# Splitting the rows once, early, for every gather, and adding them onto the sum during the routing

## The chip, the cores and the metric

The kernel runs on one core of a Trainium2 chip. The metric is the device time of one execution in microseconds, as the median of several runs. The core has five engines that run their own instruction streams and wait for each other through semaphores: TensorE (PE, matrix products; PEld is its weight loads), VectorE (DVE), ScalarE (ACT), GpSimd (POOL) and SyncE (SP), which here issues nearly all DMA transfers. Matrix products land in PSUM, eight banks of 128 partitions by 512 float32; everything else lives in SBUF.

## What is computed

One encoder layer on 256 rows of 1024 features, then a mixture of 16 small experts. Cut to what matters:

```python
h = h + (g_sb * y_sb + g_ret * y_ret) @ w_out[layer]      # output projection: the "rows" are this h
hn = rms_norm(h, norm_ffn_g[layer])
# inside the mixture, xt is hn, 256 x 1024
p_group, g_sel = lax.top_k(group_probs, 1)                 # best of 4 groups
top_vals, top_idx = lax.top_k(in_group, TOP_K_IN_GROUP)    # best 2 of its 4 experts
for e in range(N_EXPERTS):
    hidden = jax.nn.silu(xt @ w_exp_gate[e]) * (xt @ w_exp_up[e])
    y = y + combine[:, e:e + 1] * (hidden @ w_exp_down[e])
h = h + y
return rms_norm(h, norm_final_g)
```

Each row goes to two of the 16 experts.

## The kernel before

**Stages.** The input projections, attention, retention and the output projection come first. The output projection `wo` is worked off in 8 units of 256 columns by half the depth; its result is added to `xt`, a tile of 256 rows by 1024 columns in float32 (the rows). Columns 0 to 255 are finished first, then 256 to 511, and so on; the four pieces are numbered n = 0 to 3, and `tb` (0 or 1) is the half of the rows. The last piece is worked out by hand after the unit loop, together with the routing: the row norm (`row_norm`, its power on POOL), the comparison of the logits (`choose`), the ranks of the rows in each expert (small products into the PSUM tile `rp`) and the one-hot table `pt0` that says which row goes to which place.

**Experts.** They are worked off in 8 pairs, i = 0 to 7. For a pair there are three products, each of 32 matmuls of 512 columns on four weight tiles r = 0 to 3: `gate(i)`, `up(i)` and `down(i)`, L1000 and L1034 in the profile. I write g3, u3, d3 for those of pair 3. Every one of the three writes one PSUM bank, which is then read: g by the `silu` on ACT (L1010), u by the product with it on DVE (L1015), d by `hilo`, a copy on ACT (L563) and after it a subtraction on DVE (L564). The order is g0, u0, then for i = 1 to 3 g(i), d(i-1), u(i); then the second gather, d3, g4, u4; then g5, d4, u5, g6, d5, u6, g7, u7; then d6, d7 and the final norm. The banks come from a pool `g` of two one-bank tiles, so a product writes into the bank that was read after the product before the last one.

**Gathers.** The rows of eight experts are fetched into `xgt` by products with the one-hot table. For the first half of the experts this happens in float32 straight from `xt` (`gather_two`, L933): two pairs' rows (i = 0) in four pieces around g0, the other two pairs' (i = 1) in pieces around g1. For the second half it is done from `hn`, the rows split in a high and a low part of the faster matmul type (`gather`, L922). The split is made by `rows_in_parts` (ACT L944, DVE L945) during u2.

**Sum.** Four PSUM banks `F` collect the experts' results by `scatter` (L1044), and the rows themselves by `rows_onto` (L1051), in u3.

**Weights.** `pump` issues the transfer of the next weight tile (1 MiB) on SP whenever one of 25 SBUF slots is free; the table `LIMIT` says how many tiles may be on their way by which unit of the first part. Tiles from the 38th on are expert weights. `xt`, `xgt` and the two tiles of `hn` hold a slot each. `keep_warm` (L205) are products without a use, ahead of the first gather. `values_load` reads the largest number of rows of an expert into a register of every engine; it is read at the end, to choose whether one pass is enough.

Of the kernel before, what the change touches and what calls it, by code (L numbers as in the profile page):

```python
# [17 lines left out]
P = 128  # L18
T = 256
# [79 lines left out]
def layer(ctx: ExitStack, tc, cst, dec, prm, x, w_in, w_gate, w_sb_out, w_ret_out,  # L99
# [8 lines left out]
    banks = ExitStack()  # L108
    banks.__enter__()
    ps_z = banks.enter_context(tc.tile_pool(name="ps_z", bufs=1, space=PSUM))  # L110
    pp = {"d": banks.enter_context(tc.tile_pool(name="ps_d", bufs=4, space=PSUM)),
          "m": banks.enter_context(tc.tile_pool(name="ps_m", bufs=2, space=PSUM))}
# [312 lines left out]
    def squares(n, eng, tbs=range(NB)):  # L425
        cs = wo_cols[n]
        for tb in tbs:
            j, v, a = bank("d")[:, 0:cs.stop - cs.start], xt[:, tb, cs], ssh[:, n, tb:tb + 1]
# [329 lines left out]
    give(A["yrh"], A["yrl"])  # L758
    lp = bank2()
    nu = len(units)  # L760
    while i < nu - 1:
        set_limit(i)
        mm_unit(i)
        i += 1
        if i == n1 + 3:
            transpose_h(0)
            squares(0, act)
        if i == n1 + 4:
            logits(lp, 0)
        if i == n1 + 5:  # L770
            transpose_h(1)
            squares(1, act)
        if i == nu - 2:
            give(splits[(i - 1) % 3])
            logits(lp, 1)
        if i == nu - 1:
            give(splits[(i - 1) % 3], comb[0])
            transpose_h(2)
            squares(2, act)
            for n in (1, 2):  # L780
                pool.tensor_tensor(ssh[:, 0, :], ssh[:, 0, :], ssh[:, n, :], op=ALU.add)
            pool.tensor_scalar(ssh[:, 0, :], ssh[:, 0, :], 1.0 / D, EPS, op0=ALU.mult, op1=ALU.add)
# [11 lines left out]
    rp = bank("d")  # L794
# [77 lines left out]
    pt0 = small([P, NB, 4, CAP], F32R, "pt")  # L872
    onehot_of(pt0, 0, 0, ranks, 0, 2)
# [3 lines left out]
    keep_warm(1)  # L877
    onehot_of(pt0, 0, 1, ranks, 0, 2)
    give(comb[1], splits[i % 3])
    xgt = take([P, KC, T])  # L880
    limit[0] = 10 ** 6
    pump()
    dve.tensor_copy(rank, ranks)
    for tb in range(NB):
        onehot_of(pt0, 0, tb, rank, 2, 4)
# [11 lines left out]
    banks.close()  # L897
    banks = ExitStack()
    banks.__enter__()
    ctx.push(banks)  # L900
    pp["f"] = banks.enter_context(tc.tile_pool(name="ps_f", bufs=4, space=PSUM, reuse_waits="tile"))
    pp["g"] = banks.enter_context(tc.tile_pool(name="ps_g", bufs=2, space=PSUM, reuse_waits="tile"))
    pp["x"] = banks.enter_context(tc.tile_pool(name="ps_x", bufs=2, space=PSUM, reuse_waits="tile"))

# [4 lines left out]
    y2, work, gs = [], {}, {}  # L909
    F = [[bank("f") for _ in range(NB)] for _ in range(2)]  # L910
# [4 lines left out]
    def gather(k, pt, cs=range(4)):  # L915

        for c2 in cs:
            ps = bank("x").rearrange("p (c s) -> p c s", c=2)
            for h in range(2):
                for c in range(2):  # L920
                    for tb in range(NB):
# [6 lines left out]
    def gather_two(i, pt, c2):  # L928

        ps = bank("x")[:, 0:2 * P].rearrange("p (c s) -> p c s", c=2)  # L930
        for c in range(2):
            for tb in range(NB):
                pe.matmul(ps[:, c, :], xt[:, tb, features(c2, c)],  # L933
                          pt[:, tb, 2 * i:2 * i + 2].rearrange("p e s -> p (e s)").bitcast(F32),
                          start=c == 0 and tb == 0, stop=c == 1 and tb == 1, skip_group_check=True)
        tt(xgt[:, 2 * c2:2 * c2 + 2, i * P:i * P + P], ps,
           fp[:, 2 * c2:2 * c2 + 2][:, :, None].to_broadcast([P, 2, P]), op=ALU.mult)

    def rows_in_parts():
        hi, lo = hn  # L940
        for q in range(2):
            for tb in range(NB):
                cs = slice(512 * q, 512 * q + 512)
                act.activation(hi[:, tb, cs], xt[:, tb, cs], AF.Copy)  # L944
                tt(lo[:, tb, cs], xt[:, tb, cs], hi[:, tb, cs].bitcast(F32), op=ALU.subtract)  # L945
        give(xt)
# [8 lines left out]
    def tables(i):  # L955

        pb = work["pb"].rearrange("p (b e s) -> p b (e s)", b=NB, e=2)
        gp = bank("x")[:, 0:9]
# [7 lines left out]
        ps = bank("x", BF16)  # L966
# [4 lines left out]
    def convert(key):  # L971
        if len(hn) < 2 and key in (("u", 2, 0), ("u", 2, 2)):
            hn.append(take([P, NB, D], F32R))
            if len(hn) == 2:
                rows_in_parts()

    def after(key):
        drop(key)
        if not work and key == ("u", 0, 0):
            w = take([P, 2048])  # L980
            work.update(b=w[:, 0:512], ht=[w[:, 512 + 512 * k:1024 + 512 * k].rearrange("p (f s) -> p f s", f=4)
                                           for k in range(2)],
                        pb=w[:, 1536:1664].bitcast(BF16), S=[small([P, T], F32R, "S")])
        if not y2 and key == ("u", 0, 3):
            w = take([P, 2048], F32R)
            y2.append(w[:, 0:1024].rearrange("p (h n) -> p h n", h=2))
            work["S"].append(w[:, 1024:1024 + T])
        convert(key)
        pump()
# [14 lines left out]
    def gate(i, hook=None):  # L1004
        g = bank("g")
        proj(i, "g", g, hook)
        return g
# [4 lines left out]
    def up(i, hook=None):  # L1012
        u = bank("g")
        proj(i, "u", u, hook)
        stt(work["b"], u, gs[i][:, 0:1], work["b"], op0=ALU.mult, op1=ALU.mult)  # L1015

    def hidden(i):
        hps = bank("x").rearrange("p (f s) -> p f s", f=4)
# [4 lines left out]
    def down(i, hook=None):  # L1023

        y, ht = bank("g"), work["ht"][i % 2]
# [13 lines left out]
    def scatter(i, tb, first=False, last=False):  # L1039

        for h in range(2):
            for q in range(2):
                r = slice(64 * q, 64 * q + 64)
                pe.matmul(F[q][tb], work["S"][i % 2][r, tb * P:(tb + 1) * P], y2[0][r, h, :],  # L1044
                          start=first and h == 0, stop=last and h == 1, skip_group_check=True)

    def rows_onto():
        for tb in range(NB):
            for h in range(2):
                for q in range(2):  # L1050
                    pe.matmul(F[q][tb], identr, hn[h][:, tb, 512 * q:512 * q + 512], start=False, stop=False,  # L1051
                              skip_group_check=True)
# [42 lines left out]
    def head(first):  # L1095

        pt = pt0 if first else onehot(0)
        fetch = (lambda c2: gather_two(0, pt, c2)) if first else (lambda c2: gather(0, pt, [c2]))
        parts = shares() if first else iter(())
        fetch(0)  # L1100

        def ahead(r):
            if r < 3:
                fetch(r + 1)
            next(parts, None)
# [10 lines left out]
        if first:  # L1116
            gather_two(1, pt, 0)
            gather_two(1, pt, 1)
        for i in range(1, NP):
# [6 lines left out]
            def in_up(r):  # L1126
                if r == 2 and i < NP - 1:
                    for tb in range(NB):
                        scatter(i - 1, tb, first and i == 1)
                    if first and i == 3:  # L1130
                        rows_onto()
# [13 lines left out]
            if first and i == 1:  # L1145
                gather_two(1, pt, 2)
                gather_two(1, pt, 3)
# [21 lines left out]
    def final_gain(q):  # L1169
        if len(final) < 2:  # L1170
            if not final:
                final.append(take([P, 2048])[:, 0:D])
            ps = bank("x")
# [31 lines left out]
    most = nc.values_load(cnt[0:1, 0:1], min_val=0, max_val=T)  # L1205
# [3 lines left out]
    with tc.If(most <= CAP) as fits:  # L1209
# [41 lines left out]
```

## Time and profile before

| what | us |
|---|---|
| median of 3 runs (lowest to highest) | 467.12 (466.46 to 469.71) |
| the profiled execution, its own time | 468.08 |
| its span in the trace | 466.1 |

The durations below come from the profiled execution, which is 0.96 us above the median; 1.98 us of its time lie outside its span. The first gather begins at 251.97 us and the final norm at 455.7 us; between them the experts take 204 us.

### The profile page before, as it was taken

How to read it: one execution, taken by the hardware profiler on the slowest of the kernel's cores; microseconds unless marked ns; L12 is line 12 of the kernel's file. 1: busy time of each engine (PE TensorE's matmuls, PEld its weight loads, DVE VectorE, ACT ScalarE, POOL GpSimd, SP SyncE). 2: the span in 40 equal slices, each digit the busy share in tenths (PEclk: the TensorE clock that was granted, in tenths of full speed). 3: DMA queues.
4: the chain of work that ended last, by engine and by line, in shares of the span. 5: the costliest groups of instructions: out<-in, count | busy, mean ns of one | idle time of the engine just before them, and what ended most of it. 6: DMA issues, size and time to landing. Idle time of an engine off the chain costs nothing.

```text
span 466.1 us, 6780 instructions
## 1 busy us (share of the span) xinstructions
PE 446.3 (96%) x2735; PEld 301.4 (65%) x2735; DVE 187.5 (40%) x353; ACT 165.7 (36%) x239; POOL 21.8 (5%) x36
## 2 busy tenths in 40 slices
PE   7899999999999999999998999999989999999991
PEld 6699777888899999999996444333344333333330
DVE  4756487553466855678525320103012110101003
ACT  3643688885644654444431021012101010101113
POOL 2300110110002100000000000000000000000000
PEclk9999999999999999999998999999999999999996
DMA  8999985249202289995994989999999999999952
GB/s 283 353 383 392 389 258 160 84 148 317 68 8 85 92 279 380 408 377 183 356 358 190 333 323 373 412 408 411 408 409 408 410 408 409 408 410 409 409 231 96
DMA packets 58036, 142.48 MB, mean 306 GB/s; under 512 B 3344, under 2 KB 23952, under 8 KB 57872
## 3 DMA queue, kind: packets, MB, share of 16 engines
q1 hardware_dynamic: 57568, 141.35, 80.8%
q10 hardware_dynamic: 432, 0.65, 0.5%
q8 instruction: 23, 0.38, 0.3%
q14 instruction: 13, 0.11, 0.1%
HBM read 140.93 MB, written 1.05 MB: 305 GB/s over the span
## 4 chain that ended last, share of the span: by engine, by line
PE 93%; DVE 2%; ACT 1%; DMA 1%; issue 1%; POOL 1%; DVEq 0%
PE p L1000 24%; PE p L294 20%; PE p L1034 12%; PE p L281 8%; PE p L284 7%; PE p L282 7%; PE p L933 2%; PE p L1044 2%; PE z L577 1%; PE p L922 1%; PE p L1020 1%; DMA b<-in_x 1%; PE p L205 1%; PE p L679 1%; PE p L620 1%
## 5 line engine op out<-in xcount | busy, mean ns | idle before, releaser
L253 DVE TENSOR_TENSOR b<-b,b 128x1024 fp32r<-128x1024 f32 x72 | 88.7, 1240 | 71.8 <-ACT b L251 70.2
L1000 PE MATMUL p<-b,b 128*64 128x512 f32 x512 | 115.1, 596 | 0.0
L294 PE MATMUL p<-b,b 128*128 128x512 f32 (+1 forms) x504 | 102.4, 359 | 0.9 <-ACT b L251 0.7
L251 ACT ACTIVATE b<-b 128x1024 fp32r<-128x1024 f32 x72 | 75.5, 1056 | 77.3 <-PE p L282 47.8
L294 PEld LDWEIGHTS p<-b,b 128*128 128x128 f32 x504 | 82.3, 189 | 15.2 <-ACT b L251 1.3
L1000 PEld LDWEIGHTS p<-b,b 128*64 128x64 f32 x512 | 35.0, 137 | 66.3 <-issue 63.0
L281 PE MATMUL p<-b,b 128*128 128x256 f32 x288 | 71.6, 286 | 0.0
L282 PE MATMUL p<-b,b 128*128 128x256 f32 x288 | 70.7, 283 | 0.0
L1034 PE MATMUL p<-b,b 128*64 128x512 f32 x256 | 56.7, 594 | 0.0
L281 PEld LDWEIGHTS p<-b,b 128*128 128x128 f32 x288 | 55.1, 191 | 0.5
L282 PEld LDWEIGHTS p<-b,b 128*128 128x128 f32 x288 | 55.2, 192 | 0.0
L284 PE MATMUL p<-b,b 128*128 128x256 f32 x288 | 41.1, 283 | 0.0
L1034 PEld LDWEIGHTS p<-b,b 128*64 128x64 f32 x256 | 18.0, 137 | 35.1 <-issue 33.1
L564 DVE SCALAR_TENSOR_TENSOR b<-p,b 128x512 fp32r<-128x512 f32 (+1 forms) x12 | 7.2, 599 | 75.2 <-ACT b L563 75.2
L284 PEld LDWEIGHTS p<-b,b 128*128 128x128 f32 x288 | 37.4, 192 | 0.0
L1015 DVE SCALAR_TENSOR_TENSOR b<-p,share,b 128x512 f32<-128x512 f32 x8 | 6.0, 750 | 55.9 <-PE p L1000 55.9
L563 ACT ACTIVATE b<-p 128x512 fp32r<-128x512 f32 (+1 forms) x12 | 6.3, 522 | 53.4 <-PE p L1034 52.8
L969 ACT ACTIVATE b<-p 128x256 fp32r<-128x256 bf16 x4 | 1.5, 385 | 37.4 <-PE p L968 37.4
L969 ACT ACTIVATE S<-p 128x256 fp32r<-128x256 bf16 x4 | 1.5, 383 | 36.8 <-PE p L968 36.8
L1010 ACT ACTIVATE b<-p,share 128x512 f32<-128x512 f32 x8 | 5.5, 687 | 21.2 <-PE p L1000 21.2
L1021 ACT ACTIVATE b<-p 128x512 f32<-128x512 f32 x8 | 4.8, 597 | 22.9 <-PE p L1020 22.9
L933 PEld LDWEIGHTS p<-pt,b 128*128 128x128 f32 x64 | 7.9, 196 | 4.9 <-issue 4.9
(175 smaller groups left out, 342.8 us busy)
## 6 DMA issues: line engine op xcount, KB each, us to landing
b<-in_w_exp_gate SPq DMA_DIRECT2D x64, 512.0 KB, 10.2
b<-in_w_exp_up SPq DMA_DIRECT2D x64, 512.0 KB, 10.2
b<-in_w_exp_down SPq DMA_DIRECT2D x31, 1024.0 KB, 11.5
b<-in_w_in SPq DMA_DIRECT2D x17, 1024.0 KB, 14.4
b<-in_w_gate SPq DMA_DIRECT2D x8, 1024.0 KB, 5.3
b<-in_w_ret_out SPq DMA_DIRECT2D x4, 1024.0 KB, 5.0
b<-in_w_out SPq DMA_DIRECT2D x4, 1024.0 KB, 11.5
b<-in_w_sb_out SPq DMA_DIRECT2D x2, 1024.0 KB, 8.8
```

Of the source, the lines that this page charges most:

```text
L251: act.activation(hi, raw, AF.Copy)
L253: tt(lo, raw, hi.bitcast(F32), op=ALU.subtract)
L281: pe.matmul(ps, wh[:, k, cs], h[:, k, :], start=k == 0, stop=False)
L282: pe.matmul(ps, wh[:, k, cs], l[:, k, :], start=False, stop=False)
L284: pe.matmul(ps, wl[:, k, cs], h[:, k, :], start=False, stop=k == nk - 1)
L294: pe.matmul(ps[tb], kth(a, k)[:, tb * P:(tb + 1) * P], b[:, j, :], start=n == 0 and k == 0, stop=n == 2 and k == KC - 1)
L563: act.activation(hi, src, AF.Copy)
L564: stt(lo, src, 1.0, hi.bitcast(F32), op0=ALU.mult, op1=ALU.subtract)
L933: pe.matmul(ps[:, c, :], xt[:, tb, features(c2, c)], pt[:, tb, 2 * i:2 * i + 2].rearrange("p e s -> p (e s)").bitcast(F32), start=c == 0 a ...
L1000: pe.matmul(ps[64 * j:64 * j + 64, :], xgt[:, c, o:o + 64], w[:, j, k, :], start=c == 0, stop=c == KC - 1)
L1034: pe.matmul(y[64 * q:64 * q + 64, :], ht[:, f, 64 * j:64 * j + 64], w[:, k, 512 * q:512 * q + 512], start=r == 0 and k == 0, stop=r == 3 a ...
L1044: pe.matmul(F[q][tb], work["S"][i % 2][r, tb * P:(tb + 1) * P], y2[0][r, h, :], start=first and h == 0, stop=last and h == 1, skip_group_c ...
```

## The change

- `row_parts(n, tb)` splits a piece of the rows as soon as the output projection has delivered it: a copy to the high part on ACT and a subtraction for the low part on POOL, eight times in all, 128 by 256 each. `rows_in_parts`, `gather_two` and the slots taken in u2 are gone; `xgt` and the two tiles of `hn` take their slots at the start of `wo` instead, and `LIMIT` is lower there by two or three tiles.
- All gathers use the split rows, for four pairs of experts at a time: the first one stands wholly ahead of and inside g0.
- `rows_onto(q, tb)` adds the rows to the sum `F` during the routing, where the `keep_warm` products stood. It opens the sum, so `scatter` no longer does.
- The PSUM pools stay open to the end. `F` are the four `d` banks; `bank("m")` takes the place of `bank("x")`; the ranks `rp` are a corner of `lp`; and the three products of a pair write in turn into the two halves `lp[:, 0]` and `lp[:, 1]` of the one two-bank tile `lp` (`bank_g`).
- `squares` writes its unused output to SBUF. `pump` is let loose before the ranks are known, and `values_load` stands after g2.

```diff
-    (59, 48), (61, 49), (63, 50), (64, 53), (65, 54), (67, 55), (69, 56), (70, 57), (71, 59),
+    (59, 48), (61, 49), (63, 50), (65, 51), (67, 52), (69, 53), (70, 54), (71, 56),
...
+    def row_parts(n, tb):
+
+        hi, lo = [t[:, tb, wo_cols[n]] for t in hn]
+        act.activation(hi, xt[:, tb, wo_cols[n]], AF.Copy)
+        pool.tensor_tensor(lo, xt[:, tb, wo_cols[n]], hi.bitcast(F32), op=ALU.subtract)
...
     give(A["yrh"], A["yrl"])
+    xgt = take([P, KC, T])
+    junk = xgt[:, 0:2, :]
+    hn.extend(take([P, NB, D], F32R) for _ in range(2))
     lp = bank2()
...
             transpose_h(2)
             squares(2, act)
+            for tb in range(NB):
+                row_parts(2, tb)
             for n in (1, 2):
                 pool.tensor_tensor(ssh[:, 0, :], ssh[:, 0, :], ssh[:, n, :], op=ALU.add)
...
-    rp = bank("d")
+    rp = lp[:, 0, 64:96]
...
+    give(comb[1], splits[i % 3])
+    F = [[bank("d") for _ in range(NB)] for _ in range(2)]
+
+    def rows_onto(q, tb):
+        for h in range(2):
+            pe.matmul(F[q][tb], identr, hn[h][:, tb, 512 * q:512 * q + 512], start=h == 0, stop=False,
+                      skip_group_check=True)
+
     best, norm = choose(0), row_norm(1)
     next(best)
     next(norm)
+    row_parts(3, 0)
     next(best)
     next(norm)
     next(best)
+    row_parts(3, 1)
+    give(xt)
+    limit[0] = 10 ** 6
+    pump()
+    rows_onto(0, 0)
     logits(lp, 3, [1])
     pe.matmul(rp[:, 0:8], tri, either[:, 0, :], start=True, stop=True)
     pe.matmul(rp[:, 8:16], ones, either[:, 0, :], start=True, stop=False)
-    keep_warm(6)
+    rows_onto(0, 1)
+    rows_onto(1, 0)
     list(choose(1))
...
-    banks.close()
...
-    pp["g"] = banks.enter_context(tc.tile_pool(name="ps_g", bufs=2, space=PSUM, reuse_waits="tile"))
...
+    def bank_g():
+        turn[0] ^= 1
+        return lp[:, turn[0], :]
...
-        fetch = (lambda c2: gather_two(0, pt, c2)) if first else (lambda c2: gather(0, pt, [c2]))
...
+            if first and i == 2:
+                most.append(nc.values_load(cnt[0:1, 0:1], min_val=0, max_val=T))
```

The change moves instructions at three places that matter below. The first is TensorE at the borders u1 to g2, g2 to d1 and d1 to u2. A row is the line, the operation, what it writes and reads, and the semaphores that it waits for (DMAHW: a weight tile has landed; a count of ACT or DVE: an instruction there is done). Before:

```order
L1000 MATMUL p_2734<-b_2300,b_2460 64x512 x2
L1000 MATMUL p_2771<-b_2345,b_2460 64x512 [waits DMAHW0_49,PE_49]
...
L1000 MATMUL p_2771<-b_2542,b_2460 64x512 x2
L1034 MATMUL p_2817<-b_2560,b_2596 64x512 [waits DMAHW0_49,Activation_49]
...
L1034 MATMUL p_2817<-b_2604,b_2596 64x512 x3
L1000 MATMUL p_2845<-b_2622,b_2460 64x512 [waits DMAHW4_49,Activation_49]
```

After (line numbers are those of the changed kernel: L990 is g and u, L1024 is d):

```order
L990 MATMUL z_2087<-b_2419,b_2084 64x512 x2
L990 MATMUL z_2087<-b_2422,b_2084 64x512 [waits DMAHW0_49,DVE_49]
...
L990 MATMUL z_2087<-b_2527,b_2084 64x512 x2
L1123 TENSOR_LOAD cnt_2456 [waits DVE_49]
L1024 MATMUL z_2087<-b_2550,b_2567 64x512 [waits DMAHW0_49,Activation_49]
...
L1024 MATMUL z_2087<-b_2593,b_2567 64x512 x3
L990 MATMUL z_2087<-b_2607,b_2084 64x512 [waits DMAHW4_49,DVE_49]
```

All products now write one tile, `z_2087` (`lp`), and the counts have other owners. In the program before, the count at the start of d1 is that of the copy of the hidden rows at r = 2 of g2, and the count at the start of u2 that of the `silu` of g2; g2 waits for no other engine. In the changed program g2 waits for the DVE product of u1 (L1005, the L1015 of before), d1 for the `silu` of g2 (L1000, before L1010), and u2 for the subtraction of `hilo` of d1 (L568, before L564): each for the read of the product just ahead of it.

The second place is POOL in the routing. `ssh` are the sums of squares, `rh` the power that the row norm needs, for tb = 0 and 1. Before:

```order
L781 TENSOR_TENSOR ssh_91<-ssh_91 128x2 [waits Activation_49]
L781 TENSOR_TENSOR ssh_91<-ssh_91 128x2 [waits Activation_49,Pool_49]
L782 TENSOR_SCALAR ssh_91<-ssh_91 128x2 [waits Pool_49]
L820 TENSOR_TENSOR rh_2351<-rh_2351,mhalf_84 128x1 [waits DVE_49] x2
L1205 TENSOR_LOAD cnt_2470 [waits DVE_49]
```

After (L436 is the subtraction of `row_parts`; the first row here is that of n = 2, tb = 1):

```order
L436 TENSOR_TENSOR b_2086<-b_74,b_2085 128x256 [waits DMAHW5_49,DVE_49,Activation_49]
L794 TENSOR_TENSOR ssh_91<-ssh_91 128x2
L794 TENSOR_TENSOR ssh_91<-ssh_91 128x2 [waits Pool_49]
L795 TENSOR_SCALAR ssh_91<-ssh_91 128x2 [waits Pool_49]
L833 TENSOR_TENSOR rh_2351<-rh_2351,mhalf_84 128x1 [waits DVE_49]
L436 TENSOR_TENSOR b_2086<-b_74,b_2085 128x256 [waits Activation_49]
L833 TENSOR_TENSOR rh_2351<-rh_2351,mhalf_84 128x1 [waits DVE_49]
L436 TENSOR_TENSOR b_2086<-b_74,b_2085 128x256 [waits Activation_49]
```

The subtractions of n = 2 now stand ahead of the sums, and that of n = 3, tb = 0 ahead of the second power.

The third place is TensorE from the last ranks to g0. Before:

```order
L205 MATMUL p_2454<-ones_78 128x128
L1205 TENSOR_LOAD cnt_2470 [waits DVE_49]
L933 MATMUL p_2505<-pt_2449,b_74 128x128 [waits PE_49]
L933 MATMUL p_2505<-pt_2449,b_74 128x128 [waits DVE_49]
L933 MATMUL p_2505<-pt_2449,b_74 128x128 x2
L933 MATMUL p_2512<-pt_2449,b_74 128x128 x4
L1000 MATMUL p_2511<-b_1472,b_2460 64x512 [waits DMAHW4_49,DVE_49]
```

After (L879 is `rows_onto`, L939 the gather from the split rows):

```order
L879 MATMUL p_2405<-b_2085,identr_80 128x512 [waits Activation_49]
L879 MATMUL p_2405<-b_2086,identr_80 128x512 [waits Pool_49]
L939 MATMUL p_2461<-pt_2444,b_2085 128x256 [waits PE_49]
L939 MATMUL p_2461<-pt_2444,b_2085 128x256
L939 MATMUL p_2461<-pt_2444,b_2086 128x256 x2
L939 MATMUL p_2461<-pt_2444,b_2085 128x256 [waits DVE_49]
L939 MATMUL p_2461<-pt_2444,b_2085 128x256
L939 MATMUL p_2461<-pt_2444,b_2086 128x256 x2
L939 MATMUL p_2471<-pt_2444,b_2085 128x256 [waits PE_49]
```

The load of the register is gone from here, and the rows' last piece is put onto the sum ahead of the gather.

## Rows read from the trace of the kernel before

**Rows 1.** The page: busy time of the engines, and the chain by engine.

```profile
PE 446.3 (96%) x2735; PEld 301.4 (65%) x2735; DVE 187.5 (40%) x353; ACT 165.7 (36%) x239; POOL 21.8 (5%) x36
...
PE 93%; DVE 2%; ACT 1%; DMA 1%; issue 1%; POOL 1%; DVEq 0%
```

**Rows 2.** Stretches: us, busy PE, PEld, DVE, ACT, POOL, clock, DMA share, GB/s.

```profile
400.00:420.00 20.00, 19.87 (x100) 6.93 (x98) 1.20 (x5) 2.26 (x4) 0.00 (x0) 1.00 1.03 409
...
450.00:451.00 1.00, 1.00 (x6) 0.29 (x4) 0.00 (x0) 0.00 (x0) 0.00 (x0) 1.00 0.14 57
```

**Rows 3.** The timeline at u2, d2 and d6: products, and reads of those before them.

```profile
313.29 3.60 PE L1000 MATMUL p<-b,b 128*64 128x512 f32 x16
313.57 0.60 ACT L563 ACTIVATE b<-p 128x512 fp32r<-128x512 f32 x1 [6.24 <-PE p L1034]
...
314.20 0.69 DVE L564 SCALAR_TENSOR_TENSOR b<-p,b 128x512 fp32r<-128x512 f32 x1 [11.54 <-ACT b L563]
...
329.51 7.04 PE L1034 MATMUL p<-b,b 128*64 128x512 f32 x32
329.73 0.69 ACT L1010 ACTIVATE b<-p,share 128x512 f32<-128x512 f32 x1 [3.00 <-PE p L1000]
...
437.86 3.60 PE L1034 MATMUL p<-b,b 128*64 128x512 f32 x16
...
438.13 0.75 DVE L1015 SCALAR_TENSOR_TENSOR b<-p,share,b 128x512 f32<-128x512 f32 x1 [12.08 <-PE p L1000]
```

**Rows 4.** The timeline at the last scatter, which waits for the read of d7.

```profile
454.45 0.69 DVE L564 SCALAR_TENSOR_TENSOR b<-p,b 128x512 fp32r<-128x512 f32 x1 [7.31 <-ACT b L563]
...
455.19 0.96 PE L1044 MATMUL p<-b 64*128 64x512 f32 x6 [0.23 <-DVE b L564]
```

**Rows 5.** The timeline at the second half of u0.

```profile
267.32 3.65 PE L1000 MATMUL p<-b,b 128*64 128x512 f32 x16
...
267.83 1.28 ACT L1010 ACT_TABLE_LOAD   x1
...
269.12 0.69 ACT L1010 ACTIVATE b<-p,share 128x512 f32<-128x512 f32 x1
```

**Rows 6.** Weight loads of g and u, by form: busy us, mean ns.

```profile
L1000 PEld LDWEIGHTS p<-b,b 128*64 128x64 f32 x512 | 35.0, 137 | 66.3 <-issue 63.0 <-DMA b<-in_w_exp_up 1.3 <-DMA b<-in_w_exp_gate 0.7
```

**Rows 7.** The chain that ended last: start us, us, what; gathers, rows, the last product.

```profile
270.97 2.08 PE p L933 x16
...
341.11 2.05 PE p L1051 x8
...
347.93 2.42 PE p L922 x16
...
351.12 2.20 PE p L922 x16
...
448.47 5.33 PE p L1034 x24
```

**Rows 8.** The timeline of the routing, to the first gather.

```profile
242.82 0.19 POOL L782 TENSOR_SCALAR ssh<-ssh 128x2 f32<-128x2 f32 x1
...
244.02 0.16 DVE L819 SCALAR_TENSOR_TENSOR rh<-ssh 128x1 f32<-128x1 f32 x1 [0.46 <-DVE p L432]
...
246.50 0.55 POOL L820 TENSOR_TENSOR rh<-rh,mhalf 128x1 f32<-128x1 f32 x1 [1.69 <-DVE rh L819]
...
251.97 2.12 PE L933 MATMUL p<-pt,b 128*128 128x128 f32 x16 [1.41 <-DVE cnt L895]
```

**Rows 9.** Nearest forms to the split on ACT and POOL: busy us, mean ns.

```profile
L395 ACT ACTIVATE b<-b 128x256 fp32r<-128x256 f32 x8 | 3.2, 403 | 2.1 <-DVE b L389 2.1
...
L504 POOL TENSOR_TENSOR b<-b,b 128x512 fp32r<-128x512 f32 x3 | 4.1, 1372 | 7.9 <-ACT b L501 7.9
```

**Rows 10.** Stretches where TensorE stood still at times; columns as in rows 2.

```profile
247.50:250.90 3.40, 3.06 (x32) 2.79 (x29) 1.96 (x10) 0.00 (x0) 0.00 (x0) 0.50 0.79 311
...
455.00:459.00 4.00, 0.96 (x6) 0.48 (x6) 2.34 (x8) 3.10 (x9) 0.84 (x2) 1.00 0.02 4
```

More of the change, by code (lines that the diff above doesn't have):

```diff
@@ L107, in layer @@
     sm = ctx.enter_context(tc.tile_pool(name="sm", bufs=1))
[L108 to L112, printed above, removed]
+    ps_z = ctx.enter_context(tc.tile_pool(name="ps_z", bufs=1, space=PSUM))
+    pp = {"d": ctx.enter_context(tc.tile_pool(name="ps_d", bufs=4, space=PSUM)),
+          "m": ctx.enter_context(tc.tile_pool(name="ps_m", bufs=2, space=PSUM))}
     ctx.enter_context(tc.manual_schedule())
@@ L427, in squares @@
         for tb in tbs:
-            j, v, a = bank("d")[:, 0:cs.stop - cs.start], xt[:, tb, cs], ssh[:, n, tb:tb + 1]
+            j, v, a = junk[:, tb, :], xt[:, tb, cs], ssh[:, n, tb:tb + 1]
             if eng is act:
@@ L772, in layer @@
             squares(1, act)
+            for tb in range(NB):
+                row_parts(1, tb)
         if i == nu - 2:
@@ L779, in layer @@
             squares(2, act)
+            for tb in range(NB):
+                row_parts(2, tb)
             for n in (1, 2):
@@ L876, in layer @@
     pe.matmul(rp[:, 16:24], ones, either[:, 1, :], start=False, stop=True)
[L877 to L882, printed above, removed]
+    rows_onto(1, 1)
+    onehot_of(pt0, 0, 1, ranks)
     dve.tensor_copy(rank, ranks)
-    for tb in range(NB):
-        onehot_of(pt0, 0, tb, rank, 2, 4)
     sel = small([P, NB, 4], F32, "sel")
@@ L908, in layer @@
     cmb = small([P, NB, NP, 3, 3], BF16, "cmb")
-    y2, work, gs = [], {}, {}
-    F = [[bank("f") for _ in range(NB)] for _ in range(2)]
+    y2, work, gs, turn = [], {}, {}, [0]
+    def bank_g():
+        turn[0] ^= 1
+        return lp[:, turn[0], :]
     def features(c2, c):
@@ L917, in gather @@
         for c2 in cs:
[L918 to L921, printed above, removed]
+            ps = bank("m").rearrange("p (c s) -> p c s", c=2)
+            for tb in range(NB):
+                for h in range(2):
+                    for c in range(2):
                         pe.matmul(ps[:, c, :], hn[h][:, tb, features(c2, c)], pt[:, tb].rearrange("p e s -> p (e s)"),
@@ L926, in gather @@
                fp[:, 2 * c2:2 * c2 + 2][:, :, None].to_broadcast([P, 2, 2 * P]), op=ALU.mult)
[L928 to L946, printed above, removed]
     def places(i):
@@ L957, in tables @@
         pb = work["pb"].rearrange("p (b e s) -> p b (e s)", b=NB, e=2)
-        gp = bank("x")[:, 0:9]
+        gp = bank("m")[:, 0:9]
         for tb in range(NB):
@@ L965, in tables @@
             tt(g[r, 0:1], g[r, 2 + j:3 + j], g[r, 1:2], op=ALU.mult)
-        ps = bank("x", BF16)
+        ps = bank("m", BF16)
         for tb in range(NB):
@@ L969, in tables @@
         act.activation(work["S"][i % 2], ps[:, 0:T], AF.Copy)
[L971 to L975, printed above, removed]
     def after(key):
@@ L1004, in gate @@
     def gate(i, hook=None):
-        g = bank("g")
+        g = bank_g()
         proj(i, "g", g, hook)
@@ L1012, in up @@
     def up(i, hook=None):
-        u = bank("g")
+        u = bank_g()
         proj(i, "u", u, hook)
@@ L1017, in hidden @@
     def hidden(i):
-        hps = bank("x").rearrange("p (f s) -> p f s", f=4)
+        hps = bank("m").rearrange("p (f s) -> p f s", f=4)
         for f in range(4):
@@ L1023, in down @@
     def down(i, hook=None):
-        y, ht = bank("g"), work["ht"][i % 2]
+        y, ht = bank_g(), work["ht"][i % 2]
         for r in range(4):
@@ L1037, in down, with scatter @@
         hilo(y2[0][:, 0, :], y2[0][:, 1, :], y)
-    def scatter(i, tb, first=False, last=False):
+    def scatter(i, tb, last=False):
         for h in range(2):
@@ L1044, in scatter @@
                 pe.matmul(F[q][tb], work["S"][i % 2][r, tb * P:(tb + 1) * P], y2[0][r, h, :],
[L1045 to L1052, printed above, removed]
+                          start=False, stop=last and h == 1, skip_group_check=True)
     def shares():
@@ L1097, in head @@
         pt = pt0 if first else onehot(0)
-        fetch = (lambda c2: gather_two(0, pt, c2)) if first else (lambda c2: gather(0, pt, [c2]))
         parts = shares() if first else iter(())
-        fetch(0)
+        gather(0, pt, [0])
         def ahead(r):
             if r < 3:
-                fetch(r + 1)
+                gather(0, pt, [r + 1])
             next(parts, None)
@@ L1115, in head @@
         up(0, early)
-        if first:
-            gather_two(1, pt, 0)
-            gather_two(1, pt, 1)
         for i in range(1, NP):
@@ L1128, in in_up @@
                     for tb in range(NB):
-                        scatter(i - 1, tb, first and i == 1)
-                    if first and i == 3:
-                        rows_onto()
+                        scatter(i - 1, tb)
                 if r == 2 and i == NP - 1:
@@ L1144, in head @@
             silu(i, g)
-            if first and i == 1:
-                gather_two(1, pt, 2)
-                gather_two(1, pt, 3)
+            if first and i == 2:
+                most.append(nc.values_load(cnt[0:1, 0:1], min_val=0, max_val=T))
             if i != 4 and i < NP - 1:
@@ L1172, in final_gain @@
                 final.append(take([P, 2048])[:, 0:D])
-            ps = bank("x")
+            ps = bank("m")
             for k in range(4):
@@ L1203, in finish @@
             sp.dma_start(out[0, tb * P:(tb + 1) * P, halves[1]], o[:, tb, halves[1]])
-    most = nc.values_load(cnt[0:1, 0:1], min_val=0, max_val=T)
+    most = []
     head(True)
@@ L1208, in layer @@
     kept = (dict(raws), dict(held), list(free))
-    with tc.If(most <= CAP) as fits:
+    with tc.If(most[0] <= CAP) as fits:
         tail()
```

9 lines of the change are left out of this document (2 added, 7 removed).

## The prediction

> **What bounds the kernel now.** I read the page first. TensorE is busy 96% of the span and 93% of the chain that ended last is its work [rows 1], so a time is won or lost where TensorE's own queue gets shorter or stands still. Next I read the stretches of the expert phase for the transfers. From 400 to 420 us the DMA engines are as full (share 1.03, 409 GB/s) as TensorE; they run dry just after 450 us [rows 2], and the last quarter of d7, the last 8 of the 24 matmuls of its row, starts a third of 5.33 us before their end at 453.8, at 452.0 us [rows 7]. So the weights arrive only 1 to 2 us ahead of their use: TensorE bounds the kernel, and the transfers stand right behind it. Third, the timeline at the borders between the products of a pair. Here the reader should look at start times: u2 starts at 313.29 while ACT begins to read d1 only at 313.57 and DVE ends at 314.89; d2 starts at 329.51 while the silu of g3 runs from 329.73; d6 starts at 437.86 while DVE reads u7 from 438.13 [rows 3]. No product waits for the read of the one before it.
>
> **The new waits.** This is where the change decides. In the order of the changed program every product of a pair writes a half of one tile, `lp`, and its first matmul waits for the read of the other half just ahead of it. The two halves are two banks, so the data don't ask for it; the wait is in the program all the same, and a read of a product can't be done before the product is. What one costs is read from rows 3 as the end of the read, less the time at which the next product starts today. From the end of a read to the matmul that waits for it pass 0.05 us (455.14 to 455.19) [rows 4].
> - After d, before u (or g4, d7): hilo ends at 314.89, plus 0.05, less 313.29: 1.65 us. Seven such borders (u1, u2, u3, g4, u5, u6, d7): 11.5 us.
> - After g, before d (or u4, u7): the silu ends at 330.42, plus 0.05, less 329.51: 0.96 us. Seven (d0, d1, d2, u4, d4, d5, u7): 6.7 us.
> - After u, before g (or d6): the product ends at 438.88, plus 0.05, less 437.86: 1.07 us. Seven (g1, g2, g3, g5, g6, g7, d6): 7.5 us.
> - Once, in the middle of u0: its third quarter waits for the silu of g0, which stands behind a table load. Today TensorE goes on at 267.32 and the silu ends at 269.81 [rows 5]; 2.54 us.
>
> The sum is 28.3 us, all on the path, since behind the waiting matmul stands the whole of TensorE's queue, and SP's next weight transfers wait for slots that this queue frees. Bounds: at least the reads' own durations count (1.29, 0.69 and 0.75 us seven times [rows 3], and 1.97 for the load and the silu [rows 5]), 21.1 us; at most each of the 22 restarts also pays a weight load that is covered today, 0.14 us [rows 6], 31.4 us. I take 28.3, because rows 3 show the very borders.
>
> **What the gathers give back.** Removed are eight pieces of `gather_two`: 2.12 us for the first two [rows 8] and 2.08 for each further two [rows 7], 8.4 us, all on the chain. Added are four pieces of `gather`, as the two later pairs of pieces show it: half of 2.42 to half of 2.20 each [rows 7], together 4.6. The result is 3.8 us less. The rows onto the sum leave u3: 2.05 us less [rows 7]. Where they go, TensorE waits for the routing, so there they replace warm-up products and cost nothing as long as POOL is in time. The split itself leaves ACT and DVE in u2, where neither is on the path; no gain.
>
> **The routing.** Eight copies on ACT at 0.40 us (the form is in the trace) and eight subtractions on POOL, 128 by 256; the nearest row is 128 by 512 at 1.37 us [rows 9], so 0.69 to 1.37. Five of the eight are hidden beside the last units of `wo`. Three are not. Those of n = 2 stand ahead of the sums of squares: today the sums end at 243.01 and DVE asks for them at 244.02 [rows 8]; two copies and two subtractions (the second copy beside the first subtraction) put 1.8 us ahead of them and the first sum, 0.3, no longer lies earlier, so they end near 245.1, a delay of 1.1 for DVE. The next subtraction stands ahead of the second power and, behind its own copy, adds some 0.5, so that the power begins near 248.1 instead of 246.50 [rows 8]. Against these 1.6 us stands TensorE's wait of 1.41 us for the largest count ahead of the first gather, which is gone [rows 8]; the register is now read at the start of d1, beside the wait for the silu. I put the routing at nought, with bounds of 2 us less (POOL covered, the whole wait saved) and 3 us more (1.37 us a subtraction).
>
> The lower table and the slots taken early put the stock of weights three tiles lower until the routing and one lower after it. At 409 GB/s [rows 2] a tile of 1 MiB takes 2.56 us, but TensorE, some 20 us late by the end, doesn't notice; without the new waits it would be the next bound. The output of `squares` in SBUF and the earlier `pump` hide beside TensorE's queue too.
>
> **Sum.** 28.3 - 3.8 - 2.05 + 0 = 22.4 us more. On the profiled execution's 468.08 us that is 490.5; it stands 0.96 above the median of 467.12, so the forecast for the median is 489.5. By the bounds: 21.1 - 3.9 - 2.05 - 2 = 13 more, and 31.4 - 3.7 - 2.05 + 3 = 28.6 more: 480 to 496.
>
> **Rivals.** *The waits cost nothing* (faster). If TensorE ran from half to half as it runs from bank to bank today, its queue would be 5.9 us shorter, and the transfers would become the bound: they end just after 450 us and the last quarter of d7 follows at 452.0 [rows 2, 7], so 1 to 2 us are to be had, plus or minus one tile's 2.56 us for the changed stock. That gives 465, and 463 to 468 with the stock. It decides if the wait is met before TensorE's queue gets there, which would need reads shorter than TensorE's run-ahead of 0.2 to 0.3 us [rows 3]; they are 0.69 and more. For it speaks that the two halves are different banks, as they are today. The Trainium skill, "PSUM — Partial Sum Buffer", section "PSUM bank collisions raise a hardware error", asks only that accesses be guarded by bank and quadrant, and its summary advises to read a different bank while a matmul runs. The trace of before agrees (rows 3 show such reads beside matmuls), and by that rule alone a reader would forecast this rival's 465; but the rule says what the chip needs, and the program waits for more. I give it 5 in 100, and 3 in 100 to something in between, within 1%.
>
> *The clock falls* (slower still). In the routing TensorE's granted clock went to 0.50 of full, 1.2 of 2.4 GHz, for the 3.4 us from 247.5 [rows 10], after stretches with short products and waits. If each of seven pairs brought one such spell, at half speed each would cost 1.7 us: 12 us on top, 501. Against it: from 455 to 459 us TensorE is busy for 0.96 of 4 us and the granted clock is still 1.00 [rows 10], and no new wait is longer than 2.54 us. The Trainium skill, "TensorE: Matmul & The Clock Gate", section "HAM oscillation — how this bites in real kernels", describes loops that lose the clock again in every turn while TensorE waits for data, which is this case; rows 10 speak for and against. 6 in 100 beyond 496.
>
> *The routing is the loss.* If POOL held the routing up by 3 us and the new waits were met, 468 to 471 would come out; it is the in-between case, and the waits on TensorE would be short in the trace.
>
> **How the numbers follow.** The forecast, with its bounds, has 84 in 100, the clock 6, the waits that cost nothing 5, the in-between cases 3, and 2 remain for less than 480 with the waits in force. The range is that of the forecast, 480 to 496, which leaves about 16 out. A change of 1% is about what a measurement of this kernel tells from none: faster by more than that (below 462.4) 3, within it 5 (most of the first rival lies here), slower 92.
>
> **What would show it.** In the trace after, TensorE's idle time in the expert phase should be put down to DVE and ACT on the first matmul of each product, about 22 times, at 1 to 1.7 us, some 25 us in all, where today it has almost none; the DMA share should fall from 1.03 to about 0.9 between 300 and 440 us; the granted clock should stay at 1.00 there; the first gather should begin near 252 us and g1 about 1 us later than today. The prediction is wrong if d(i-1), u(i) and g(i) follow each other without a gap, or if the gaps are there and the clock falls too.

## The result and the profile after

| what | before | after |
|---|---|---|
| median, us (lowest to highest) | 467.09 (466.46 to 469.71) | 492.40 (491.22 to 494.03) |
| profiled execution, us | 468.08 | 491.26 |
| its span, us | 466.1 | 489.4 |

Four runs each. The ratio is 1.0533, with a 95% interval from 1.0477 to 1.0589: 25.3 us slower, where 22.4 were forecast. The forecast of 489.5 (480 to 496) holds the time. Line numbers below are those of the changed kernel: L990 is g and u, L1024 is d, L1000 the `silu`, L1005 the product with it, L567 and L568 the two parts of `hilo`, L939 the gather, L1034 `scatter`.

The page, its busy time and the chain, against [rows 1]:

```profile
PE 446.7 (91%) x2675; PEld 295.3 (60%) x2675; DVE 185.0 (38%) x343; ACT 166.3 (34%) x243; POOL 27.7 (6%) x44
...
PE 88%; DVE 4%; ACT 3%; issue 2%; DMA 1%; POOL 1%; SPq 0%; ACTq 0%; DVEq 0%; POOLq 0%
```

TensorE has 60 matmuls fewer and is busy as long as before, but the span is 23 us longer: time in which it stands. DVE and ACT have come onto the chain, with 7% in place of 3%. For whom TensorE waits is said by its waits in the expert phase (253 to 480 us): who waits for whom, us in total, times, the longest:

```profile
PE z L990 <- DVE b L568: 9.1, 6, 1.8
PE z L990 <- DVE b L1005: 5.2, 6, 0.9
PE z L990 <- ACT b L1000: 4.0, 3, 2.5
PE z L1024 <- ACT b L1000: 3.9, 5, 0.8
PE z L1024 <- DVE b L568: 1.5, 1, 1.5
...
PE z L1024 <- issue: 1.0, 1, 1.0
```

That is 22 waits and 24.7 us. The last line, "issue", is d6 behind u7, which stands beside no releaser that the profile knows. The timeline shows one pair; TensorE alone in the first fence, the readers of d1 in the second, as [rows 3] showed them before:

```profile
301.99 3.65 PE L990 MATMUL z<-b,b 128*64 128x512 f32 x16 [0.85 <-DVE b L1005]
...
311.07 7.09 PE L1024 MATMUL z<-b,b 128*64 128x512 f32 x32 [0.79 <-ACT b L1000]
319.64 3.65 PE L990 MATMUL z<-b,b 128*64 128x512 f32 x16 [1.48 <-DVE b L568]
...
328.85 1.08 PE L990 MATMUL z<-b,b 128*64 128x512 f32 x4 [0.85 <-DVE b L1005]
```

```profile
318.26 0.60 ACT L567 ACTIVATE b<-z 128x512 fp32r<-128x512 f32 x1 [7.25 <-PE z L1024]
318.89 0.69 DVE L568 SCALAR_TENSOR_TENSOR b<-z,b 128x512 fp32r<-128x512 f32 x1 [12.55 <-ACT b L567]
```

These are g2, d1, u2 and g3. d1 ends at 318.16; its two reads run until 319.58, and u2 starts 0.06 us later. The same stretch of before: first the second halves of g2 and g3 in its chain (and the start of g1, which is used further below), then the second half of g3 in its timeline.

```profile
273.06 3.58 PE p L1000 x16
...
303.01 3.58 PE p L1000 x16
...
326.10 3.58 PE p L1000 x16
```

```profile
326.03 3.65 PE L1000 MATMUL p<-b,b 128*64 128x512 f32 x16
```

From g2 to g3 pass 26.86 us in the changed kernel. In the kernel before, 23.09 us pass from the second half of g2 to that of g3, which is one pair as well: 3.77 more, against 0.96 + 1.65 + 1.07 = 3.68 in the prediction. The idle time alone is less, 0.79 + 1.48 + 0.85 = 3.12 us. Where no product waits, the next one begins a little before the last matmul of the one ahead ends in the trace (before: g3 until 329.68, d2 from 329.51 [rows 3]), and a wait takes this overlap away too: 0.79 + 0.17 = 0.96 for a d behind a g.

The second half of u0, in the timeline, and below it stretches as in [rows 2]:

```profile
266.88 1.28 ACT L1000 ACT_TABLE_LOAD   x1
268.17 0.69 ACT L1000 ACTIVATE b<-z,share 128x512 f32<-128x512 f32 x1
...
268.91 5.35 PE L990 MATMUL z<-b,b 128*64 128x512 f32 x16 [2.47 <-ACT b L1000]
...
275.17 0.65 PE L990 MATMUL z<-b,b 128*64 128x512 f32 x2 [0.91 <-DVE b L1005]
```

```profile
269.00:272.40 3.40, 3.40 (x10) 0.98 (x12) 0.00 (x0) 0.00 (x0) 0.00 (x0) 0.58 0.46 187
...
400.00:420.00 20.00, 17.53 (x88) 5.83 (x86) 2.32 (x7) 1.58 (x3) 0.00 (x0) 1.00 1.03 409
450.00:451.00 1.00, 0.54 (x4) 0.26 (x6) 0.00 (x0) 0.40 (x1) 0.00 (x0) 1.00 1.03 410
...
300.00:440.00 140.00, 122.80 (x598) 42.66 (x594) 15.03 (x41) 11.34 (x20) 0.00 (x0) 1.00 1.03 409
```

The wait of 2.47 us is there as forecast, and behind it TensorE's clock is at 1.2 of 2.4 GHz for some 3 us: the 16 matmuls take 5.35 us instead of 3.65 [rows 5]. The last line is the start of g1. From 300 to 440 us the clock stays at 1.00, through the waits of the pairs. From 400 to 420 us TensorE is busy 17.5 of 20 us where it was 19.9, and the DMA engines are as full as before.

The routing, against [rows 8]:

```profile
242.86 1.60 POOL L436 TENSOR_TENSOR b<-b,b 128x256 fp32r<-128x256 f32 x2 [5.63 <-ACT b L435]
...
245.20 0.16 DVE L832 SCALAR_TENSOR_TENSOR rh<-ssh 128x1 f32<-128x1 f32 x1 [1.33 <-POOL ssh L795]
...
247.68 0.56 POOL L833 TENSOR_TENSOR rh<-rh,mhalf 128x1 f32<-128x1 f32 x1
...
251.01 2.08 PE L939 MATMUL p<-pt,b 128*128 128x256 f32 x16
```

POOL takes 1.60 us for two subtractions, DVE gets the sums of squares 1.18 us later than before and the second power is 1.18 us later; the first gather begins 0.96 us earlier, at 251.01.

### The profile page after: what moved, and what is told of

It reads as the page before. It is cut to its first block, busy times and chain, and to the rows that moved or that the text cites. A ratio compares the mean times of both kernels' runs of the same rounds, so it can differ in the third digit from the quotient of the medians.

```text
span 489.4 us, 6673 instructions
## 1 busy us (share of the span) xinstructions
PE 446.7 (91%) x2675; PEld 295.3 (60%) x2675; DVE 185.0 (38%) x343; ACT 166.3 (34%) x243; POOL 27.7 (6%) x44
## 2 busy tenths in 40 slices
DMA packets 58037, 142.48 MB, mean 291 GB/s; under 512 B 3345, under 2 KB 23953, under 8 KB 57873
## 3 DMA queue, kind: packets, MB, share of 16 engines
HBM read 140.93 MB, written 1.05 MB: 290 GB/s over the span
## 4 chain that ended last, share of the span: by engine, by line
PE 88%; DVE 4%; ACT 3%; issue 2%; DMA 1%; POOL 1%; SPq 0%; ACTq 0%; DVEq 0%; POOLq 0%
PE z L990 24%; PE p L292 20%; PE z L1024 12%; PE p L279 7%; PE p L282 7%; PE p L280 7%; PE p L939 2%; PE p L1034 2%; PE z L581 1%; DMA b<-in_x 1%; DVE b L568 1%; ACT b L1000 1%; DVE b L1005 1%; ACT b L567 1%; PE p L1010 1%
## 5 line engine op out<-in xcount | busy, mean ns | idle before, releaser
L990 PE MATMUL z<-b,b 128*64 128x512 f32 x512 | 118.6, 606 | 18.4 <-DVE b L568 9.1
L990 PEld LDWEIGHTS z<-b,b 128*64 128x64 f32 x512 | 34.3, 138 | 90.9 <-issue 57.4
L1024 PE MATMUL z<-b,b 128*64 128x512 f32 x256 | 57.1, 596 | 6.4 <-ACT b L1000 3.9
L1024 PEld LDWEIGHTS z<-b,b 128*64 128x64 f32 x256 | 17.7, 137 | 43.9 <-issue 32.4
L568 DVE SCALAR_TENSOR_TENSOR b<-z,b 128x512 fp32r<-128x512 f32 x8 | 5.5, 692 | 87.8 <-ACT b L567 87.8
L1005 DVE SCALAR_TENSOR_TENSOR b<-z,share,b 128x512 f32<-128x512 f32 x8 | 6.0, 751 | 75.3 <-PE z L990 75.3
L567 ACT ACTIVATE b<-z 128x512 fp32r<-128x512 f32 x8 | 4.8, 597 | 57.7 <-PE z L1024 57.7
L1173 POOL TENSOR_TENSOR rf<-rf,mhalf 128x1 f32<-128x1 f32 x2 | 1.1, 542 | 232.9 <-DVE rf L1172 232.9
L1011 ACT ACTIVATE b<-p 128x512 f32<-128x512 f32 x8 | 4.8, 598 | 23.6 <-PE p L1010 23.6
L1000 ACT ACTIVATE b<-z,share 128x512 f32<-128x512 f32 x8 | 5.5, 688 | 21.2 <-PE z L990 21.2
```

What stands on the lines that cost most here:

```text
L568: stt(lo, src, 1.0, hi.bitcast(F32), op0=ALU.mult, op1=ALU.subtract)
L990: pe.matmul(ps[64 * j:64 * j + 64, :], xgt[:, c, o:o + 64], w[:, j, k, :], start=c == 0, stop=c == KC - 1)
L1000: act.activation(work["b"], g, AF.Silu, scale=gs[i][:, 1:2])
L1024: pe.matmul(y[64 * q:64 * q + 64, :], ht[:, f, 64 * j:64 * j + 64], w[:, k, 512 * q:512 * q + 512], start=r == 0 and k == 0, stop=r == 3 a ...
```

## The experiments

**The wait alone.** The kernel before, with one edit: the products write in turn into the two halves of one two-bank tile instead of two one-bank tiles.

```diff
-    pp["g"] = banks.enter_context(tc.tile_pool(name="ps_g", bufs=2, space=PSUM, reuse_waits="tile"))
+    ps_g = banks.enter_context(tc.tile_pool(name="ps_g", bufs=1, space=PSUM, reuse_waits="tile"))
+    gg, turn = ps_g.tile([P, 2, 512], F32, name="gg", tag="gg"), [0]
...
+    def bank_g():
+        turn[0] ^= 1
+        return gg[:, turn[0], :]
...
-        g = bank("g")
+        g = bank_g()
```

(and so for u and y)

> The kernel before with one edit: the products of a pair write into the two halves of one two-bank tile. Theory A: the same 22 waits come in, two of them (at g1 and d0) covered by the pieces of the gather that stand there, so 28.3 less 2.0 is 26.3 us, and perhaps 1.8 us for a low clock after the long wait in u0: 493 to 496 us for the median against 467.1. Theory B: within 2 us of the kernel before, since neither POOL nor the stock of weights is changed.

Measured: 495.18 us (494.18 to 496.27), ratio 1.0582 (1.0540 to 1.0624). Its waits, of those from 253 to 480 us (L1005 is g and u there, L1039 d, L564 the end of `hilo`, L1020 the product, L1015 the `silu`):

```profile
PE gg L1005 <- DVE b L564: 8.8, 6, 1.5
PE gg L1005 <- DVE b L1020: 5.1, 5, 1.6
PE gg L1005 <- ACT b L1015: 4.0, 3, 2.5
PE gg L1039 <- ACT b L1015: 3.2, 4, 0.8
```

As expected, 20 waits came in and not 22; they last 23.6 us in all, two of them in lines not shown here. The one edit makes the whole loss and more; the rest of the change gives some of it back. Both profiled executions have one spell of low clock, in u0, and they took 495.80 and 491.26 us: 4.5 us given back, where 5.9 of gathers and rows less 2.0 for the two covered waits are 3.9. The first gather and g0 of this run are of use as well, since nothing of the routing was changed here:

```profile
250.93 2.12 PE L938 MATMUL p<-pt,b 128*128 128x128 f32 x16 [1.62 <-DVE cnt L895]
252.98 1.94 PE L1005 MATMUL gg<-b,b 128*64 128x512 f32 x8
```

In this execution the clock didn't fall during the routing, and g0 begins at 252.98. In the profiled execution of before, with its spell at half clock [rows 10], it began at 254.02. The changed kernel's g0 begins at 253.02, without such a spell.

**Everything but the wait.** The changed kernel, with two one-bank tiles for the products. `lp` is given back behind the routing and a pool of two banks opened in its place. The other six banks are taken to the end, so these are the same two banks as in the changed kernel, with the same matmuls and the same readers.

```diff
-    ps_z = ctx.enter_context(tc.tile_pool(name="ps_z", bufs=1, space=PSUM))
...
+    banks = ExitStack()
+    banks.__enter__()
+    ps_z = banks.enter_context(tc.tile_pool(name="ps_z", bufs=1, space=PSUM))
...
+    banks.close()
+    banks = ExitStack()
+    banks.__enter__()
+    ctx.push(banks)
+    pp["g"] = banks.enter_context(tc.tile_pool(name="ps_g", bufs=2, space=PSUM, reuse_waits="tile"))
...
-        turn[0] ^= 1
-        return lp[:, turn[0], :]
+        return bank("g")
```

> The changed kernel, with the three products of a pair writing in turn into two one-bank tiles of a pool, as before the change, instead of the two halves of lp; all else as changed. Theory A (the first matmul of each product waits for the read of the other half of the one tile): the 22 waits go, some 28 us, and the low clock in u0 with them; what stays is what the change gives back (3.9 us of gathers, 2.05 us of rows, 1.0 us in the routing), but the weights then bound the end: 463 to 466 us for the median against 467.1 of before. Theory B (the loss comes from POOL in the routing, from the lower stock of weights or from the clock, and the waits only mark it): 485 us or more.

Measured: 467.19 us (465.63 to 469.08, 12 runs), ratio 0.9993 (0.9972 to 1.0014). The wait is the loss: without it 25 us are gone. Two of its waits in the expert phase (L1030 is d there, L569 the copy of `hilo`), then the end of its chain (start us, us, what), then two stretches as in [rows 2]:

```profile
PE p L1030 <- DMA b<-in_w_exp_down: 1.9, 3, 0.7
...
PE p L1030 <- ACT b L569: 0.7, 1, 0.7
```

```profile
295.28 13.59 DMA b<-in_w_exp_down
...
431.94 19.10 DMA b<-in_w_exp_down
451.08 3.68 PE p L1030 x16
```

```profile
248.20:251.60 3.40, 3.14 (x11) 2.22 (x11) 2.58 (x12) 0.51 (x1) 0.92 (x2) 0.50 1.00 390
251.60:255.00 3.40, 3.40 (x17) 3.32 (x15) 0.75 (x2) 0.00 (x0) 0.00 (x0) 0.50 1.03 422
```

No product waits for the reader of the other bank any more. The line that names ACT is the start of d7, at 446.09 us. That isn't the reader's wait: d6, in the other bank, is read until 446.88 there. The start lies 2.65 us behind the last wait for a weight tile (443.44), which is the pace of the transfers. From 295 us to d7 the chain is nearly all transfers: the weights are the bound, and they end at 451.04, no earlier than before [rows 2]. The shorter queue of TensorE doesn't show. The time missed the 463 to 466 that were expected, for this and for a spell of low clock of 6.8 us in the routing and the first gather.

The Trainium skill, "PSUM — Partial Sum Buffer", section "PSUM bank collisions raise a hardware error", has the rule to guard accesses by bank and quadrant, or more simply by bank. The changed kernel and this run agree that the chip wanted no more than that: a read of one bank beside the matmuls of the other costs nothing with two tiles, and with one tile the program itself had the wait.

**The table of the silu earlier.** The changed kernel, with a one-element `silu` in the first half of u0, so that ACT loads its table there.

```diff
+                if first:
+                    act.activation(small([P, 1], F32, "early"), mhalf[:, 0:1], AF.Silu)
```

> The changed kernel with one more instruction: a silu of one element on ACT in u0, ahead of the copy of the place table, so that the table load lies beside the first half of u0 and not inside TensorE's wait. Theory A: the wait in u0 falls from 2.5 to about 1.2 us. If the low clock in the rest of u0 comes from the length of this wait, 1.8 us more are won, 489.4 us for the median of 492.4; if it comes anyway, 491.1.

Measured: 489.27 us (487.99 to 490.66), ratio 1.0450 (1.0409 to 1.0492). The timeline of u0:

```profile
269.10 0.68 ACT L1000 ACTIVATE b<-z,share 128x512 f32<-128x512 f32 x1
...
269.83 3.65 PE L990 MATMUL z<-b,b 128*64 128x512 f32 x16 [1.05 <-ACT b L1000]
```

The wait is 1.05 instead of 2.47 us, and the 16 matmuls behind it run at full clock, 3.65 us. In this profile low clock stands elsewhere, for some 7 us around the first gather. Over all runs of the two kernels the granted clock and the time go together: 487.99 and 488.37 us at 0.991 and 490.16 and 490.66 at 0.987 and 0.985 here; 491.2 twice at 0.988 and 493.5 and 494.0 at 0.981 in the changed kernel. So the executions lie 2 to 2.5 us apart by their spells. That the shorter wait is what kept u0 at full clock fits, but one profile doesn't show it.

**Half of the weights of d7.** The version with two tiles, with half of the weights of d7 not transferred and the other half used twice, so that d7 is not the layer's.

```diff
-                 [((slice(None), k), e[:, k]) for k in range(2)] if cut else [(slice(None), e)])
+                 [((slice(None), 0), e[:, 0])] if i == NP - 1 else [(slice(None), e)])
...
-  ... w[:, k, 512 * q:512 * q + 512],
+  ... w[:, k if i < NP - 1 else 0, 512 * q:512 * q + 512],
```

> As e1_two_tiles, but of the four weight tiles of the last product, d7, only one half is transferred and used twice, so that the result of d7 is not the layer's: 2 MiB less, 5.1 us at 409 GB/s, with TensorE's work unchanged. If the weights bound e1_two_tiles, this is 1 to 4 us faster than it, down to what TensorE's queue allows, about 461 us; if TensorE bounds it, the two agree within 0.5 us.

Measured: 465.87 us (464.07 to 466.23, 10 runs), ratio to before 0.9951 (0.9931 to 0.9972). It is 1.3 us faster than with all weights, the low end of what was expected. The end of its chain:

```profile
426.76 15.29 DMA b<-in_w_exp_down
442.09 3.65 PE p L1029 x16
...
446.87 5.33 PE p L1029 x24
```

Transfers are the chain here too, until d6 at 442 us; so it didn't take the bound away, and the next run takes more.

**Half of the weights of every down projection.** As the one before, for all d: 16 MiB less, the same matmuls; the experts' output is not the layer's.

```diff
-                 [((slice(None), k), e[:, k]) for k in range(2)] if cut else [(slice(None), e)])
+                 [((slice(None), 0), e[:, 0])])
...
-  ... w[:, k, 512 * q:512 * q + 512],
+  ... w[:, 0, 512 * q:512 * q + 512],
```

> This is the version with two one-bank tiles for the products, but only half of every down projection's weights is transferred and used twice, 8 MiB less in all, so that the output of the experts is not the layer's; TensorE has the same matmuls as before. Theory A (the shorter queue of TensorE is there, 3.9 us of gathers and 2.05 us of rows, and the transfers alone ate it): no wait for weights is left, and 467.1 - 5.9 - 1.0 (the earlier routing) = 460 come out if the clock holds, 462 to 463 if the spell of low clock at the first gather is there again. Rival B (the new gathers and rows onto the sum give back little by themselves): 465 to 466, as with half of d7 alone.

The 8 MiB of the expectation are a slip: half of 32 tiles of 1 MiB are 16, and the bytes moved fall from 142.48 to 125.70 MB. Measured: 460.24 us (459.65 to 460.76, 5 runs), ratio 0.9843 (0.9821 to 0.9866). Stretches at the first gather and late in the expert phase, and the last product of the chain:

```profile
249.00:251.00 2.00, 1.01 (x9) 0.93 (x9) 1.59 (x9) 0.00 (x0) 0.00 (x0) 1.00 0.99 389
...
400.00:450.00 50.00, 47.02 (x232) 16.57 (x228) 5.84 (x14) 7.50 (x17) 0.54 (x1) 1.00 0.36 141
```

```profile
440.39 5.33 PE p L1029 x24
```

TensorE has no wait for weights left (the DMA share late in the phase is 0.36), the clock holds, and d7's last row runs 8.1 us earlier than in before [rows 7]. The 460 of theory A came out. The shorter queue is there, some 6 to 7 us of it, and the transfers alone eat it. The kernel before was not run with half of these weights; its TensorE has no wait for weights in the expert phase, so little should come of it there, but that is argued.

**Keeping the clock up in the routing.** The version with two tiles, with one call of `rows_onto` (two matmuls of 512 columns) moved ahead of the ranks and 16 warm-up products behind the next.

```diff
     logits(lp, 3, [1])
+    rows_onto(0, 1)
     pe.matmul(rp[:, 0:8], tri, either[:, 0, :], start=True, stop=True)
     pe.matmul(rp[:, 8:16], ones, either[:, 0, :], start=True, stop=False)
-    rows_onto(0, 1)
     rows_onto(1, 0)
+    keep_warm(4)
```

> This is the version with two one-bank tiles for the products, in which the rows onto the sum for the second half of the first 512 columns stand ahead of the rank products instead of behind them, and 16 warm-up products stand where TensorE waited for the second set of ranks. In the version without this, TensorE's clock stood at half for 6.8 us from 248.2 us, and the first two pieces of the gather took 3.38 us. Theory A (that spell of low clock delays g0 by some 2 us, and with it the slots that g0 frees and all transfers behind them): the spell shortens, g0 begins near 253.5, the end comes 1 to 2 us earlier, 465 to 466. Rival B (the transfers end when they end, whatever g0 does): 467 again, with an earlier g0 and more waits for weights. If the clock still falls, the run tells nothing of either.

Measured: 466.41 us (465.47 to 467.60, 12 runs), ratio 0.9971 (0.9956 to 0.9986) to runs of before with a median of 467.98. The two stretches in which the version without it was at half clock, and a wait of its expert phase:

```profile
248.20:251.60 3.40, 2.71 (x29) 2.22 (x29) 2.58 (x12) 0.51 (x1) 0.93 (x2) 1.00 1.01 387
251.60:255.00 3.40, 3.40 (x22) 1.96 (x21) 2.34 (x11) 0.00 (x0) 0.00 (x0) 1.00 1.04 423
```

```profile
PE p L1031 <- DMA b<-in_w_exp_down: 2.6, 4, 0.7
```

The clock stayed at 1.00, g0 began at 253.20 instead of 255.15, and the last 16 matmuls of d7, which wait for the last weights, start at 449.62 instead of 451.08. In all 12 runs the mean granted clock is 0.990 or more. The 12 runs of the version without it fall in two halves, six at 0.985 to 0.988 with a median of 468.2 us and six at 0.989 to 0.993 with 466.1. But the two had run on different chips, and so both ran again, beside each other on one chip. First the version with two tiles:

> The version with two one-bank tiles again, beside the one with the rows in the gap on the same chip, since the two were timed on different chips before. Theory A (the order of products in the routing sets the spells of low clock): about half of its executions are at a mean granted clock below 0.989 and near 468, and its median is 0.5 to 2 us above the other's. Rival B (the spells are the chip's and the day's, not the order's): both have the same share of such executions, and the medians agree within 0.4 us.

And the one with the moved and added products:

> The version with one product of the rows ahead of the ranks and 16 warm-up products, on the same chip as the version without. Theory A: all its executions are at a mean granted clock of 0.989 or more, 465.5 to 467.6 us, and its median is 0.5 to 2 us below the other's. Rival B: the two agree within 0.4 us.

Measured: 467.36 us (465.78 to 468.93, 12 runs), ratio 0.9994 (0.9975 to 1.0013), without; 466.59 us (465.22 to 467.76, 12 runs), ratio 0.9974 (0.9957 to 0.9992), with. Without them six of the 12 executions are again at 0.986 to 0.988, with them all are at 0.990 or more, so theory A holds for the clock: the products keep the spells away. The time is less sure: the medians are 0.8 us apart, inside the 0.5 to 2 expected, but the two intervals overlap. They bring no more, because a run without a spell is bound by the transfers at some 466 us with or without them. This version is the fastest that computes the layer, by 0.3% against the kernel before, and its gain is the clock's, not the gathers': the kernel before has the spells too, and of its 23 runs beside these, the ten at 0.991 or more have a median of 466.9 us and the 13 at 0.990 or less one of 468.6.

## Why the prediction was right

**The waits** were the step that decided, and it was right in kind and size. The run with that edit alone is 5.8% slower and the run without it is at par, so the cause is shown from both sides. The size: 3.77 us a pair where 3.68 were summed, and in u0 2.47 us idle where 2.54 were. "Some 25 us idle, about 22 times" was 24.7 in 22 waits, most of them 0.8 to 1.5 us long; with the overlap of some 0.17 us that each of them takes away, an estimate from the border of g3 and d2, they cost 24.7 + 3.7 = 28.4 us, against 28.3 in the sum.

**The clock** was a rival, and one spell of it came true. It was priced at 1.7 us; the one in u0 cost 5.35 - 3.65 = 1.7. It did not come back with each pair: from 300 to 440 us the clock is 1.00, so the rival's 501 was far off. Two of the four runs have a lower mean clock and are 2.5 us longer, and this puts the median 1.1 us above the profiled execution.

**The routing at nought** held, though the trace alone seems to give 1 us back. POOL's delay was 1.18 us where 1.6 were summed (the eight subtractions took 0.76 on average, in the lower part of 0.69 to 1.37). But the 0.96 us by which the first gather comes earlier is the spell of low clock that the profiled execution of before had [rows 10] and this one has not: the kernel before with only the one tile, without a spell, begins g0 at 252.98, the changed one at 253.02.

**The sum**, on the profiled executions: 7 x 3.77 + 2.5 for the waits, 1.7 for the clock in u0, 1.0 less for the clock in the routing, 3.8 less for the gathers and 2.05 less for the rows: 23.7; measured were 489.4 - 466.1 = 23.3.

**The gathers and the rows** were sized well as work of TensorE (5.9 us; 460.24 without the bound of the transfers), and in the changed kernel they count in full, since there TensorE is the bound. In the rival where the waits cost nothing they were held to be worth 1 to 2 us, to 465. Measured were 467.19, inside its 463 to 468, and 466.1 in the runs with the higher clock: all of it is eaten. The step that was too kind there is "1 to 2 us are to be had", read from the time between the end of the transfers and d7's last quarter in before; the transfers didn't end earlier with g0 as late as it was, and the last 16 matmuls of d7 start when their weights land.

**Two signs were off.** g1 was to begin about 1 us later and began 2.1 later (275.17 instead of 273.06); 1.7 of this is the spell in u0. And the DMA share was to fall to 0.9 between 300 and 440 us. It stayed at 1.03 there. A pair takes 12 tiles of 1 MiB, 12.6 MB; in 26.9 us that is 468 GB/s, still over the 409 that the engines deliver. The slots therefore kept coming free faster than they were filled, and the transfers went on at their own pace. They end near 454 us, with d7 only at 469: the late TensorE gained stock, not idle transfers. The prediction had looked at the pace of TensorE alone and not at which of the two was slower.

## What to carry to other kernels

Two halves of one tile are one thing to the program that orders the engines, even when they are two banks: a product that alternates between halves waits for the reader of the other half, so give each buffer in turn a tile of its own, and look in the order of instructions for a wait that the data don't ask for. What such a wait costs can be read beforehand: the end of the read, less the start of the next product, in the trace where they still overlap. Work taken from an engine is worth what the next bound leaves of it: here 6 us of matmuls were removed and the transfers, 1 us behind, kept them all.

## What the runs showed of the hardware

Spells at 1.2 GHz lasted some 3.4 or 6.8 us and cost 1 to 2.5 us each; they came where TensorE stood or had only short products (the routing, u0 behind a wait of 2.47 us), in some executions of a kernel and not in others, and not in the 17.2 us of idle time that lie spread from 300 to 440 us, in waits of 0.8 us and more. With two matmuls of 512 columns moved and 16 warm-up products put into the gaps of the routing no execution of 24 was below a mean clock of 0.990; without them 12 of 24 were at 0.988 or less. A subtraction on GpSimd of 128 by 256 took 0.72 to 0.92 us (eight of them, 0.76 on average), beside 1.37 for 128 by 512 [rows 9].
